# A small early store on the Scalar queue of a DMA-bound softmax

## The chip, the cores and the metric

One core of a Trainium2 chip runs the kernel. The metric is device time in microseconds (us), the median of several executions; most executions of one kernel agree within 0.3%. One traced execution of each kernel gives its profile, whose times count from the start of the span (161.2 us of the 163 us). "Before" is the kernel without the change and "after" the one with it.

## The reference

```python
def setup_inputs():
    batch, seq, dim = 16, 1024, 512
    return {"x": np.random.randn(batch, seq, dim).astype(np.float32)}

def reference(x):
    x_scaled = x / 0.5
    x_max = np.max(x_scaled, axis=-1, keepdims=True)
    exp_x = np.exp(x_scaled - x_max)
    return (exp_x / np.sum(exp_x, axis=-1, keepdims=True)).astype(np.float32)
```

It is a softmax with temperature 0.5 over 16,384 rows of 512 floats: 33.55 MB are read and 33.55 MB written.

## The kernel before

The rows are cut into 8 tiles of 4 MiB. A tile holds 128 partitions with 16 rows each, and those 16 rows lie together in memory, so one partition's share is a run of 32 KiB. Six tiles have buffers. Loads are issued from the Sync engine (SP), stores from the Scalar engine (ACT), one store for each tile.

```python
    FIRST = [(0, 4), (4, 16)]
    data = ctx.enter_context(tc.tile_pool(name="data", bufs=6))
    stats = ctx.enter_context(tc.tile_pool(name="stats", bufs=6))
    ctx.enter_context(tc.manual_schedule())

    warm = stats.tile([P, 1], fp32, name="warm", bufs=1)
    nc.vector.memset(warm, 0.0)
    nc.scalar.activation(out=warm, in_=warm, func=EXP)   # loads ACT's table
    ...
    def load(c):
        xt = tiles[c] = data.tile([P, G, D], fp32, name="xt")
        for lo, hi in FIRST if c == 0 else [(0, G)]:
            nc.sync.dma_start(out=xt[:, lo:hi, :], in_=xr[c][:, lo:hi, :])
    ...
    def store(i):
        c, b = blocks[i]
        if b + B == G:
            nc.scalar.dma_start(out=outr[c], in_=tiles[c])

    for i in range(n + 3):                 # n blocks of 4 rows per partition
        if i < n:
            if blocks[i][1] == 0:
                load(blocks[i][0])
            shift(i)                       # DVE: row maxima
            exponentials(i)                # ACT: exp, in place
        if 1 <= i <= n:
            scale_vector(i - 1)            # DVE: 3 of 4 rows
        if 2 <= i <= n + 1:
            scale_scalar(i - 2)            # ACT: the fourth row
        if 3 <= i:
            store(i - 3)
```

## Time and profile before

| | before |
|---|---|
| time, median of 3 | 162.96 us (162.91 to 163.17) |
| DVE busy / ACT busy | 74% / 71% of the span |
| bytes moved | 67.1 MB |
| first large store issued | 34.23 us |
| its first packets on the 16 DMA engines | 38.6 to 40.4 us |
| last store: first / last of 16 completions | 158.05 / 159.94 us |

These lines of the page of before show the span in 40 slices: first the busy share of the DMA engines in tenths, then what they moved. The two after them give the DMA queues (q1 is SP's, q10 is ACT's; packets, MB, share of the 16 engines' time), and the last two the chain of waits that ended last.

```profile
DMA  5999999998999999999999999999999999999991
GB/s 193 457 463 447 390 463 447 392 455 317 417 472 398 431 472 398 423 480 398 423 472 409 390 488 423 390 488 423 390 488 423 390 488 425 390 480 431 390 480 65
...
q1 hardware_dynamic: 1296, 33.56, 49.2%
q10 hardware_dynamic: 1152, 33.55, 48.2%
...
DMA 54%; DVE 31%; ACT 3%; issue 1%; SPq 0%
DMA xt<-in_x_dram 36%; DVE negmax L65 19%; DMA out_dram<-xt 18%; DVE xt L89 10%; ACT xt L74 2%; DVE bias L67 1%; ACT xt L95 1%; DVE recip L87 1%; SPq L59 0%
```

The DMA engines are busy from the second slice to the last but one: they are the bound. Whatever makes them move less for a moment should therefore be paid at the end.

The GB/s of a slice counts a packet's bytes where the packet starts, and one round of packets on 16 engines is half a megabyte, so neighbouring slices swing between 390 and 488 though nothing happens. For a finer reading I took the trace's DMA packet records and spread each packet's bytes evenly over its duration. Then before moves 433 GB/s in nearly every whole microsecond from 5 to 157 us, with one exception near the tenth slice. Here is that calculation for the microseconds from 34 to 41, in GB/s (the second row is another trace of the same kernel, taken later as an experiment):

```
microsecond      34   35   36   37   38   39   40   41
before          433  428  336  293  321  363  423  429
rep_before      433  433  362  308  310  367  419  426
```

I call this *the hole*. It has a size: the KB missing below 433 GB/s in the ten whole microseconds that follow the issue of the first large store, counted in the packets of the two data queues (q1 and q10) alone. It is 459 and 425 KB in these two traces, about 1.0 us of all 16 engines. In it, 28 to 32 load packets take 1.4 to 2.08 us instead of the usual 1.21 us.

These are the first rows of the timeline of before, and the first store's issue (start, duration, engine, line, what). ACTq and SPq are issues. The Trainium skill (Perfetto Trace Analysis, section on the HWDGE DMA instruction) says that the data movement of a DMA is not inside the reported instruction; this trace agrees: the issue takes 0.37 us and the first packet starts 4.4 us after its start.

```profile
0.72 1.28 ACT L50 ACT_TABLE_LOAD   x1 [0.72 <-PEq L131]
0.73 3.33 SPq L59 DMA_DIRECT2D xt<-in_x_dram  x7
0.80 0.06 DVE L49 MEMSET warm<- 128x1 f32 x1 [0.80 <-PEq L131]
2.02 0.20 ACT L50 ACTIVATE warm<-warm 128x1 f32<-128x1 f32 x1
5.43 2.29 DVE L65 TENSOR_REDUCE negmax<-xt 128x4 f32<-128x2048 f32 x1 [4.58 <-DMA xt<-in_x_dram]
...
34.23 0.37 ACTq L102 DMA_DIRECT2D out_dram<-xt  x1
```

### The profile page before, as it was taken

The page shows a single profiled execution, that of the slowest core. Times are in us where ns is not written, and L with a number is a line of the kernel's source. Part 1 is how long each engine was busy: PE and PEld are TensorE (multiplying, and loading weights), DVE is VectorE, ACT ScalarE, POOL GpSimd, SP SyncE. Part 2 cuts the span into 40 slices and gives each one's busy share as a digit, 9 for nine tenths or more (in the row PEclk, how much of TensorE's full clock was granted, in tenths as well). Part 3 has the DMA queues.
Part 4 walks back from the last instruction along what each step waited for, and adds up shares of the span by engine and source line. Part 5 has one row for each costly group of instructions (what it writes and reads, how often), then busy time and mean ns, then how long its engine had stood idle before and what let it go on. Part 6 is the DMA issues. An engine that isn't in the chain of part 4 may idle for free.

```text
span 161.2 us, 563 instructions
## 1 busy us (share of the span) xinstructions
DVE 119.7 (74%) x193; ACT 114.8 (71%) x290; POOL 0.2 (0%) x4
## 2 busy tenths in 40 slices
DVE  0608999999999999999994999359991799930000
ACT  3072799999999998999995799809997199980000
POOL 0000000000000000000000000000000000000000
DMA  5999999998999999999999999999999999999991
GB/s 193 457 463 447 390 463 447 392 455 317 417 472 398 431 472 398 423 480 398 423 472 409 390 488 423 390 488 423 390 488 423 390 488 425 390 480 431 390 480 65
DMA packets 2452, 67.14 MB, mean 416 GB/s; under 512 B 272, under 2 KB 272, under 8 KB 272
## 3 DMA queue, kind: packets, MB, share of 16 engines
q1 hardware_dynamic: 1296, 33.56, 49.2%
q10 hardware_dynamic: 1152, 33.55, 48.2%
q14 instruction: 4, 0.03, 0.0%
HBM read 33.55 MB, written 33.55 MB: 416 GB/s over the span
## 4 chain that ended last, share of the span: by engine, by line
DMA 54%; DVE 31%; ACT 3%; issue 1%; SPq 0%
DMA xt<-in_x_dram 36%; DVE negmax L65 19%; DMA out_dram<-xt 18%; DVE xt L89 10%; ACT xt L74 2%; DVE bias L67 1%; ACT xt L95 1%; DVE recip L87 1%; SPq L59 0%
## 5 line engine op out<-in xcount | busy, mean ns | idle before, releaser
L74 ACT ACTIVATE xt<-xt,bias 128x512 f32<-128x512 f32 x128 | 90.8, 710 | 28.9 <-DVE bias L67 28.9
L65 DVE TENSOR_REDUCE negmax<-xt 128x4 f32<-128x2048 f32 x32 | 73.0, 2281 | 19.8 <-DMA xt<-in_x_dram 19.8
L89 DVE TENSOR_SCALAR xt<-xt,recip 128x512 f32<-128x512 f32 x96 | 40.9, 483 | 1.1
L74 ACT ACTIVATION_READ_ACCUMULATOR xt<-xt,bias 128x1 f32 x128 | 23.9, 187 | 0.0
L95 ACT ACTIVATE xt<-xt,recip 128x512 f32<-128x512 f32 x32 | 22.4, 706 | 0.0
L87 DVE RECIPROCAL recip<-sums 128x4 f32<-128x4 f32 x32 | 5.5, 171 | 1.6 <-ACT xt L74 1.6
L67 DVE TENSOR_SCALAR bias<-negmax 128x4 f32<-128x4 f32 x32 | 5.5, 170 | 1.1
L50 ACT ACT_TABLE_LOAD x1 | 1.3, 1283 | 0.7 <-PEq L131 0.7
L49 DVE MEMSET warm<- 128x1 f32 x1 | 0.1, 59 | 0.8 <-PEq L131 0.8
L50 ACT ACTIVATE warm<-warm 128x1 f32<-128x1 f32 x1 | 0.2, 203 | 0.0
L131 POOL MEMSET const-bfloat16-1.0<- 128x1 bf16 x1 | 0.1, 101 | 0.0
L131 POOL MEMSET const-uint8-127<- 128x1 uint8 x1 | 0.1, 101 | 0.0
L131 POOL MEMSET const-float32-0.0<- 128x1 f32 x1 | 0.1, 98 | 0.2 <-issue 0.2
L131 POOL MEMSET const-float32-1.0<- 128x1 f32 x1 | 0.1, 98 | 0.0
## 6 DMA issues: line engine op xcount, KB each, us to landing
out_dram<-xt ACTq DMA_DIRECT2D x8, 4096.0 KB, 26.9
xt<-in_x_dram SPq DMA_DIRECT2D x7, 4096.0 KB, 47.3
xt<-in_x_dram SPq DMA_DIRECT2D x1, 3072.0 KB, 11.5
xt<-in_x_dram SPq DMA_DIRECT2D x1, 1024.0 KB, 4.7
```

Source lines behind the costliest of these rows:

```text
L49: nc.vector.memset(warm, 0.0)
L50: nc.scalar.activation(out=warm, in_=warm, func=EXP)
L65: nc.vector.tensor_reduce(negmax, xb, axis=AX, op=MAX, negate=True)
L67: nc.vector.tensor_scalar_mul(bias, negmax, 2.0)
L74: nc.scalar.activation(out=xb[:, g, :], in_=xb[:, g, :], func=EXP, bias=bias[:, g : g + 1], scale=2.0, accum_out=sums[:, g : g + 1],)
L87: nc.vector.reciprocal(recip, sums)
L89: nc.vector.tensor_scalar_mul(xb[:, g, :], xb[:, g, :], recip[:, g : g + 1])
L95: nc.scalar.activation(out=xb[:, g, :], in_=xb[:, g, :], func=COPY, scale=recip[:, g : g + 1])
L131: nc = _bacc.Bacc("TRN2", target_bir_lowering=False, num_devices=1)
```

## The change

The intent is to take the first use of the Scalar queue, with whatever it costs, out of the stretch where the DMA engines are saturated, and put it at the start, where the first load is still on its way.

```diff
+    dram = ctx.enter_context(
+        tc.tile_pool(name="dram", bufs=1, space=bass.MemoryType.DRAM)
+    )
     ctx.enter_context(tc.manual_schedule())
 
+    early = stats.tile([P, 128], fp32, name="early", bufs=1)
+    nc.vector.memset(early, 0.0)
+    scratch = dram.tile([P, 128], fp32, name="scratch")
+    nc.scalar.dma_start(out=scratch, in_=early)
+
     warm = stats.tile([P, 1], fp32, name="warm", bufs=1)
-    nc.vector.memset(warm, 0.0)
-    nc.scalar.activation(out=warm, in_=warm, func=EXP)
+    nc.scalar.activation(out=warm, in_=early[:, 0:1], func=EXP)
```

## The prediction

> **What bounds the kernel now.** The DMA engines. The page's slices show them 90% busy or more from 4 us to the end, for 67.1 MB. Spreading the trace's DMA packet records evenly over their durations gives 433 GB/s in nearly every microsecond from 5 to 157 us. In the table of groups DVE is busy 74% and ACT 71%; in the chain of waits DMA has 54%. The last store is issued at 144.5 us (timeline), while packets of the store before it run to about 150 us: compute has some 4 us of slack.
>
> The one visible hole is at the first store. It is issued on the Scalar queue at 34.23 us, its first packets start at 38.6 to 40.4 us, and meanwhile packets of the loads, 1.21 us for 32 KiB elsewhere, take 1.4 to 2.07 us. The sum falls to 290 to 360 GB/s between 36 and 40 us; about 430 KB is missing, 1.0 us of the 16 engines. It also spreads them: a load's 16 completions lie within 0.43 us before (31.27 to 31.71 us), 2.1 us after (45.5 to 47.6), and the last store's within 1.9 us (158.05 to 159.94). No later issue shows such a hole; both queues then always have work.
>
> **What the change does.** It makes a 64 KiB store the Scalar queue's first DMA, so what the first use costs falls near 1 to 4 us, where the engines are idle until 1.76 us and slow until 3 us (the first load's packets take up to 0.83 us against 0.31 later).
> Added: a memset of 128 columns instead of 1 (0.06 us now, I estimate 0.1 to 0.2); one issue of about 0.34 us on ACT ahead of the 1.28 us table load. ACT is idle until 7.96 us: free. 64 KiB is 0.15 us at 433 GB/s; in 512-byte rows perhaps 0.2 to 0.4 us. The Trainium skill (DMA: Bandwidth & Descriptors, Measured) has 0.95 us of DMA for 64 KB, from another queue; here it overlaps the load.
> Moved: the completion semaphores rotate by one. The sixth full load now waits for the first 1 MiB load (landed by 5.1 us); it was issued near 4 us behind other loads, so nothing is lost.
>
> **How much is critical.** All DMA time. If the hole belongs to the queue's first use, up to 2.1 us on the slowest engine (1.0 mean) leaves 36 to 40 us, and a smaller part, plus 0.2 to 0.4 us for the bytes, appears at the start: net gain 0.5 to 1.8 us. If it belongs to any store that starts on an idle queue while loads stream, it stays, and the change costs 0 to 0.4 us. The Trainium skill (same page, Queues, rings and completion order) gives each queue its own ring on each DMA engine; that does not tell which. I hold the first slightly likelier.
>
> **Predicted:** 162.2 us, 160.7 to 163.6 in 8 of 10 cases; faster by over 2% 0.04, within 2% 0.94, slower by over 2% 0.02.
>
> **What would show it.** Right: the first tile's store starts its packets 1 to 2 us after its issue; load packets around 36 us stay near 1.21 us; the tenth slice rises from 317 GB/s towards 400; the completions near 45 us lie within 1 us. Cost: the first maximum on DVE starts 0.2 to 1 us later than 5.43 us. Wrong: the hole near 36 us stays.
>
> **What would make it wrong.** A hole whenever a store stream begins; a full-size hole at the start, which gives the gain back; an engine left behind by chance.

## The result and the profile after

| | before | after |
|---|---|---|
| time, median | 163.06 us (162.91 to 163.21, 4 runs) | 163.08 us (162.93 to 163.47, 4 runs) |
| ratio | | 1.0005, 95% interval 0.9983 to 1.0027 |
| the 3 MiB load has landed (mean of 16 completions) | 12.07 us | 12.51 us |
| hole at the first large store | 459 KB | 324 KB |
| last store: mean / last of 16 completions | 158.56 / 159.94 us | 158.63 / 159.85 us |

A ratio is the mean time of one kernel's runs over that of the other's of the same rounds, so it is not quite the ratio of the medians quoted. The change does nothing that can be measured: the interval holds 1, and the forecast gain of 0.8 us would have been a ratio of 0.995, outside it.

The same lines of the page of after:

```profile
DMA  5999999999999999999999999999999999999992
GB/s 171 472 415 447 455 398 447 457 398 390 392 472 431 398 472 431 398 463 439 398 455 433 407 464 431 407 463 431 407 455 439 407 439 447 409 439 455 407 423 114
...
q1 hardware_dynamic: 1296, 33.56, 49.1%
q10 hardware_dynamic: 1296, 33.62, 48.4%
...
DMA 54%; DVE 31%; ACT 3%; issue 1%; SPq 0%
DMA xt<-in_x_dram 37%; DVE negmax L74 19%; DMA out_dram<-xt 18%; DVE xt L98 10%; ACT xt L83 2%; DVE bias L76 1%; ACT xt L104 1%; DVE recip L96 1%; SPq L68 0%
```

And its timeline, with the issues of the early store and of the first large store:

```profile
0.73 5.49 SPq L68 DMA_DIRECT2D xt<-in_x_dram  x7
0.82 0.17 DVE L53 MEMSET early<- 128x128 f32 x1 [0.82 <-PEq L140]
1.02 0.36 ACTq L55 DMA_DIRECT2D scratch<-early  x1
1.42 1.28 ACT L59 ACT_TABLE_LOAD   x1 [1.42 <-DVE early L53]
2.71 0.20 ACT L59 ACTIVATE warm<-early 128x1 f32<-128x1 f32 x1
5.90 2.29 DVE L74 TENSOR_REDUCE negmax<-xt 128x4 f32<-128x2048 f32 x1 [4.91 <-DMA xt<-in_x_dram]
...
34.81 0.37 ACTq L111 DMA_DIRECT2D out_dram<-xt  x1
```

The list of DMA issues of after has the early store's size and its time from issue to landing, 5.0 us:

```profile
scratch<-early ACTq DMA_DIRECT2D x1, 64.0 KB, 5.0
```

What was forecast of the added work is there: the memset takes 0.17 us, the issue 0.36 us, the table load ends at 2.70 instead of 2.00 us, and the seventh issue of SP waits for the first load (the seven issues take 5.49 instead of 3.33 us) without harm. The first maximum on DVE starts 0.47 us later.

The tenth slice has gone from 317 to 390 GB/s, which the prediction had named as a sign of success. It is not one. Counted evenly over their durations, the packets of this slice moved 330 GB/s before and 357 after; the rest of the rise comes from where packets start. The second trace of after, rep_after, also has 365 GB/s in this slice by its page, and only 311 when spread evenly. The view of windows for 36 to 40 us (busy times by engine, granted clock, DMA share, GB/s), which also counts packets where they start, says the opposite. Before has 385 GB/s there:

```profile
36.00:40.00 4.00, 3.93 (x7) 3.75 (x10) 0.00 (x0) 1.00 1.13 385
```

The same window of after has 360 GB/s:

```profile
36.00:40.00 4.00, 3.93 (x8) 3.75 (x11) 0.00 (x0) 1.00 1.01 360
```

The packet records, spread evenly, show the hole still there, in this trace and in a second one taken later:

```
microsecond      34   35   36   37   38   39   40   41     hole
after           434  434  419  388  307  324  422  433    324 KB
rep_after       434  434  373  253  264  364  417  434    509 KB
```

The first packets of the large store come 3.9 us after its issue (38.73 us), against 4.4 us before; in the second traces it is the other way round, 4.7 us for rep_after and 4.2 us for rep_before.

### The profile page after: what moved, and what is told of

It is laid out like the page before. It is cut to its first block, busy times and chain, and to the rows that moved or that the text cites. A ratio compares the mean times of both kernels' runs of the same rounds, so it can differ in the third digit from the quotient of the medians.

```text
span 161.2 us, 565 instructions
## 1 busy us (share of the span) xinstructions
DVE 119.8 (74%) x193; ACT 114.8 (71%) x290; POOL 0.2 (0%) x4
## 4 chain that ended last, share of the span: by engine, by line
DMA 54%; DVE 31%; ACT 3%; issue 1%; SPq 0%
DMA xt<-in_x_dram 37%; DVE negmax L74 19%; DMA out_dram<-xt 18%; DVE xt L98 10%; ACT xt L83 2%; DVE bias L76 1%; ACT xt L104 1%; DVE recip L96 1%; SPq L68 0%
```

## The experiments

After the first look there were three theories.

- *A, the first use*: the queue has a price of first use. The early store should have paid it, unless the queue "goes cold" again while it is idle from 5.7 to 34.8 us.
- *B, the joining store*: a hole comes whenever a stream of large stores begins, whatever the queue did before.
- *C, the joining queue*: a hole comes whenever any transfer begins on an empty queue beside a busy one.

In the expectations quoted below "missing" often refers to a fixed stretch such as 32 to 48 us; that is 15 to 30 KB more than the size of the hole as I defined it. Where I give the hole after an early store, it is that of the eight whole microseconds after its issue.

### Both kernels again (rep_before, rep_after)

No edit.

> The kernel before, unchanged, for a second profile: how far the hole at the first store and the spread of completions repeat. In the first profile about 430 KB were missing between 36 and 40 us, load 3's completions ended at 47.6 us and the last store's lay between 158.05 and 159.94 us. If these are a property of the kernel, the hole comes again within 100 KB; if the hole differs by 100 KB or more, the apparent shrinking from 430 to 310 KB in the changed kernel is noise.

> The changed kernel, unchanged, for a second profile and more times. Two profiles of the kernel before miss 482 and 450 KB between 32 and 48 us; the first profile of the changed kernel misses 351 KB there and 318 KB from 2 to 8 us (195 and 211 KB before). If the early store really buys part of the hole and gives it back at the start, this profile again misses about 350 KB at 32 to 48 us. If the smaller hole was chance, it misses about 450 KB. The time is within 0.3% of before either way.

Measured: before again (one run, 163.42 us) has a hole of 425 KB. After again took 163.34 us, ratio 1.0008 (0.9988 to 1.0029), and its hole is 509 KB. So 459 and 425 KB stand against 324 and 509 KB: the smaller hole of the first trace of after was chance. The hole is where it was. The cost at the start does repeat: the mean completion of the 3 MiB load is 12.51 and 12.46 us in the two traces of after, and between 12.07 and 12.26 us in the fourteen traces whose start is that of before: some 0.3 us of delay.

### The small store just before the large one (small_at_25)

```diff
... (early, its memset and scratch as in the change, without the store there)
     for i in range(n + 3):
+        if i == 4:
+            nc.scalar.dma_start(out=scratch, in_=early)   # the same 64 KiB
         if i < n:
```

> The 64 KiB store is moved from the start to about 25 us, so it ends only some 5 us before the first large store. Theory A (the queue was warmed, but goes cold again in the 30 us of idle time that the changed kernel leaves): the hole at 36 to 40 us shrinks to under 150 KB, and a smaller hole of 100 to 300 KB appears around 27 us. Theory B (a hole comes whenever a large store joins on an empty ring while loads stream, whatever went over the ring before): the hole at 36 to 40 us stays at 300 to 430 KB. In both the time is within 0.5% of before.

Measured: 163.18 us, ratio 1.0010 (0.9995 to 1.0025). The small store ends between 35.2 and 36.0 us, more than 12 us after its issue and after the large one has been issued at 34.32 us: its packets take turns with load packets 64 times their size. The hole after its issue is 5 KB, and the hole at the large store is 439 KB. The queue had no time to go cold, and the hole is whole: the cold-queue form of theory A falls.

### A load on the Scalar queue first (load5_on_act)

```diff
-            nc.sync.dma_start(out=xt[:, lo:hi, :], in_=xr[c][:, lo:hi, :])
+            (nc.scalar if c == 5 else nc.sync).dma_start(out=xt[:, lo:hi, :], in_=xr[c][:, lo:hi, :])
...
-            if blocks[i][1] == 0:
+            if i == 3:
+                load(5)
+            if blocks[i][1] == 0 and blocks[i][0] != 5:
```

> The sixth 4 MiB load is issued on the Scalar queue at about 23 us, so this queue has work when the first store is issued behind it at about 34 us. If the hole is the price of a large transfer joining on an empty ring (either direction), it moves to 24 to 29 us and nothing is missing at 34 to 45 us. If it is the price of the first large store (the change of direction), nothing is missing at 24 to 29 us and the hole comes when the store's packets begin, near 43 us. Time within 0.5% of before in either case, since one hole remains.

The issues on the Scalar queue, from the timeline of this run:

```profile
19.18 0.38 ACTq L59 DMA_DIRECT2D xt<-in_x_dram  x1
34.34 0.35 ACTq L102 DMA_DIRECT2D out_dram<-xt  x1
```

Measured: 162.87 us, ratio 0.9987 (0.9970 to 1.0003), which holds 1. The load joins on the empty Scalar queue, its first packet starts at 22.9 us, and the eight microseconds after its issue miss nothing (-1 KB). The store waits behind it in the queue, and the hole comes where the store's packets begin:

```
microsecond      34   35   36   37   38   39   40   41   42   43   44   45
load5_on_act    433  434  434  434  433  430  402  328  295  387  391  409
```

So it is not the queue that joins (theory C falls), nor the queue's first use by packets of 32 KiB: they had just gone through it. It is the first large store.

### The first store in smaller pieces (store0_pieces, rows_16k, rows_8k)

The first store in four stores of 8 KiB per partition:

```diff
-            nc.scalar.dma_start(out=outr[c], in_=tiles[c])
+            for lo in range(0, G, 4 if c == 0 else G):
+                hi = lo + (4 if c == 0 else G)
+                nc.scalar.dma_start(out=outr[c][:, lo:hi, :], in_=tiles[c][:, lo:hi, :])
```

and all transfers with runs of 16 KiB (H = 2) or 8 KiB (H = 4), by another assignment of rows to partitions, with the first tile's loads cut to fit:

```diff
-    xr = xf.rearrange("(c p g) d -> c p g d", p=P, g=G)
+    xr = xf.rearrange("(c h p g) d -> c p h g d", h=H, p=P, g=G // H)
...
-            nc.scalar.dma_start(out=outr[c], in_=tiles[c])
+            nc.scalar.dma_start(out=outr[c], in_=tiles[c].rearrange("p (h g) d -> p h g d", h=H))
```

> The first tile's store is issued as four stores of 4 rows per partition, 8 KiB in a row in place of 32 KiB. If the hole grows with the packet that joins (a fill or hand-over of one packet per engine), it shrinks to under 200 KB and the first store packet comes earlier than 4.4 us after the issue. If it is a fixed latency of the queue, the hole stays at 300 to 430 KB and the first store packet still comes about 4 us after the issue. Time within 0.5% of before.

> Rows are assigned to partitions so that every transfer, load or store, moves pieces of 16 KiB instead of 32 KiB. If the hole is about one store packet per engine, it halves, to 200 to 270 KB at 34 to 48 us. If it is a fixed latency at the change to stores, it stays at 400 to 480 KB. The time is within 0.5% of before: about 0.5 us less for the hole, against a slightly lower rate of smaller packets.

> The same with pieces of 8 KiB for loads and stores. If the hole is about one store packet per engine it falls to a quarter, 90 to 150 KB at 34 to 48 us, and the first store packet comes within about 3 us of its issue. If it is a fixed latency, it stays at 400 to 480 KB. The 8 KiB packets took 309 ns (26.5 GB/s for each engine against 27.0), so the time is expected 1 to 3 us longer.

Measured: store0_pieces 163.29 us, ratio 1.0022 (0.9996 to 1.0048), hole 217 KB; here it is no clean case, because the 8 KiB store packets took turns with 32 KiB load packets, the first store dragged on to 71 us, the loads ran ahead and their queue ran empty at 67 us. rows_16k 163.64 us, ratio 1.0028 (1.0011 to 1.0045), hole 342 KB. rows_8k 164.42 us, ratio 1.0078 (1.0059 to 1.0097), hole 108 KB, below its own level of 424 GB/s (some 80 to 150 KB for levels of 422 to 428, which its rate has before and after). So 8 KiB packets make the hole smaller, by about the three quarters that were expected, and it is not a fixed latency. For 16 KiB half was expected, and 342 KB lies within the 324 to 509 KB of the four traces with 32 KiB packets: one trace does not show that it shrank at all. The first store packet of rows_8k came 3.6 us after its issue, later than the 3 us expected. Neither is faster: the smaller packets run at a lower rate (8 KiB in 309 ns, 16 KiB in 611 ns, 32 KiB in 1213 ns), for the whole run.

### An early store with large packets (big_at_22, big_spread_at_22, same_bytes_4k)

From here on an early store of 512 KiB goes out from the second tile as soon as that has landed, at about 22.5 us:

```diff
+    scratch = dram.tile([16, G, D], fp32, name="scratch")
...
     for i in range(n + 3):
+        if i == 3:
+            load(1)
+            nc.scalar.dma_start(out=scratch, in_=tiles[1][0:16, :, :])      # big_at_22
+            nc.scalar.dma_start(out=scratch, in_=tiles[1][0:P:8, :, :])     # or big_spread_at_22
+            nc.scalar.dma_start(out=scratch, in_=tiles[1][:, 0:2, :])       # or same_bytes_4k, scratch [P, 2, D]
...
-            if blocks[i][1] == 0:
+            if blocks[i][1] == 0 and i != 4:
```

> At about 22 us a store of 16 rows of 32 KiB (512 KiB, one packet of full size for each DMA engine) goes over the Scalar queue to a scratch tensor, and has ended before the first large store. Theory A2 (the first use by packets of full size is what costs): a hole of 300 KB or more at 24 to 30 us and none above 150 KB at 34 to 48 us. Theory B (every time such a store starts on an idle store stream, the engines fall behind by about a packet): 300 to 450 KB missing at 34 to 48 us as before, and a hole of up to that size at 24 to 30 us too. Time: 1.2 us more for the bytes, plus up to 1 us under B.

> As the store of 16 rows of 32 KiB at 22 us, but from partitions 0, 8, 16 and so on in place of 0 to 15. The last run missed 1089 KB at 24 to 32 us, its 16 packets took 2.7 to 4.0 us each, and nothing was missing at the first large store later (38 KB). If the long packets came from 16 neighbouring partitions being read at once, the packets now take under 2.5 us and 350 to 650 KB are missing at 22 to 32 us, while still under 100 KB are missing at the first large store. The time is then about 1 to 1.5 us longer than before (1.2 us of bytes, one hole as before).

> The same 512 KiB at the same place, but as 128 rows of 4 KiB. If the amount that has gone out before counts, the first large store shows no hole (under 100 KB). If the size of a packet counts, most of the hole stays (300 KB or more at the first large store), and 22 to 32 us shows less than 200 KB missing. Time 1.2 to 2.5 us longer than before.

Measured: big_at_22 takes 166.08 us, ratio 1.0184 (1.0160 to 1.0209). Its 16 packets take 2.7 to 4.0 us each and the engines fall to 148 GB/s for two microseconds (1070 KB missing), but at the first large store only 17 KB are missing. big_spread_at_22, which reads from every eighth partition instead of 16 neighbours, takes 164.17 us, ratio 1.0058 (1.0033 to 1.0083): its packets take 1.21 us each, 355 KB are missing after its issue, and 44 KB at the first large store, which is issued at 37.55 us on a queue that has been idle since 30.2 us. Its two first issues on that queue, from the timeline, and its GB/s:

```profile
22.53 0.55 ACTq L112 DMA_DIRECT2D scratch<-xt  x1
37.55 0.38 ACTq L106 DMA_DIRECT2D out_dram<-xt  x1
```

```
microsecond        24   25   26   27   28      38   39   40   41   42   43
big_spread_at_22  369  337  305  370  434     434  433  430  417  427  433
```

This also fells theory B in its plain form: a stream of large stores that begins on an idle queue need not have a hole. same_bytes_4k takes 164.48 us, ratio 1.0083 (1.0053 to 1.0113): 13 KB are missing after its issue and 336 KB at the first large store. The same bytes in small packets do not do it. (An early store also holds ACT up until the second tile has landed, so the first large store comes later, at 36.4 to 44.1 us. That does not remove the hole: same_bytes_4k is the latest of them and has it.)

### Running empty in between (gap_big, gap_only)

Is it then something that is done once, at the first store with large packets? Or a state that holds only while the engines are kept busy? The third load is held back by a small write of DVE to its tile, so that no queue has anything to do for a while, with and without the early store of big_spread_at_22.

```diff
         xt = tiles[c] = data.tile([P, G, D], fp32, name="xt")
+        if c == 2:
+            nc.vector.memset(xt[:, 0, 0:1], 0.0)
...
+        if i == 3:
+            load(1)
+            nc.scalar.dma_start(out=scratch, in_=tiles[1][0:P:8, :, :])    # gap_big only
+        if i == 5:
+            load(2)
+            for c in range(3, 6):
+                load(c)
...
-            if blocks[i][1] == 0:
+            if blocks[i][1] == 0 and blocks[i][0] not in range(1, 6):
```

> As the spread store at 22 us, but the third load is held back by a write of the vector engine to its tile, so that all queues run empty before loads resume; some microseconds later the first large store joins. Theory L (the hole is a lead that the engines' reading takes over their writing, of one large packet, and keeps as long as the queues never run empty): the hole comes back at the first large store, 300 KB or more. Theory F (something is done once, at the first use by a large store packet): under 100 KB are missing at the first large store.

> The same gap without the early store, as a control: both theories expect the hole at the first large store, 300 KB or more missing. If it is missing here too, the gap alone removes it and the run with both says nothing.

The issues in gap_big, from its timeline:

```profile
22.66 0.55 ACTq L114 DMA_DIRECT2D scratch<-xt  x1
28.25 1.95 SPq L65 DMA_DIRECT2D xt<-in_x_dram  x4
34.48 0.38 ACTq L108 DMA_DIRECT2D out_dram<-xt  x1
```

```
microsecond      24   25   26   27   28   29   30   31   32  ...  34   35   36   37   38   39   40
gap_big         211  218   83    0    0  171  272  383  433  ... 433  431  372  329  299  382  434
```

Measured (one run each, 174.97 and 174.53 us, longer by the gap): the early store is over at 26.5 us, nothing moves for the microseconds 27 and 28, loads resume, and at the first large store 372 KB are missing; without the early store 363 KB. In big_spread_at_22, where the loads went on and the Scalar queue alone had been idle for 7 us, it did not come. So it is not something that the first store with large packets does once, whatever goes on around it.

What in gap_big brings the hole back is not shown. Its early store went out alone, because the loads' queue had been empty since 22.3 us; each of its 16 packets took 2.2 to 2.6 us, where those of big_spread_at_22, between load packets, took 1.21 us. So it may never have built what removes the hole, or what it built may have been lost in the gap. Near their end both runs have a second gap, in which no data packet moves from 147.9 to 152.0 us (147.4 to 151.6 in gap_only), and the store after it starts at once with packets of 1.21 to 1.22 us. After an emptiness that long between stores alone, then, no slow packets are seen. A run with the early store between loads and the gap after both would decide it; there is none.

### Grading it (mid_16k_at_22, mid_8k_at_22, one_16k_at_22)

The spread early store again, with other sizes. The one from 32 partitions moves two packets of 16 KiB on each engine, the one from 64 four of 8 KiB, and the third, of only 256 KiB, one of 16 KiB.

```diff
+            nc.scalar.dma_start(out=scratch, in_=tiles[1][0:P:4, 0:8, :])   # mid_16k_at_22
+            nc.scalar.dma_start(out=scratch, in_=tiles[1][0:P:2, 0:4, :])   # or mid_8k_at_22
+            nc.scalar.dma_start(out=scratch, in_=tiles[1][0:P:8, 0:8, :])   # or one_16k_at_22
```

> The spread store of 512 KiB at 22 us in pieces of 16 KiB (32 partitions). The hole at the first large store was about 325 KB after pieces of 4 KiB and under 60 KB after pieces of 32 KiB. Theory L (the lead grows only to the size of the largest store packet so far): two holes that add up to the one of before, about 150 to 250 KB at 22 to 32 us and 150 to 250 KB at the first large store. Theory F2 (only a packet of full size does it, all or nothing): over 350 KB, or under 80 KB, at the first large store. Time about 1 us longer than before either way.

> The same with pieces of 8 KiB (64 partitions). Theory L: 50 to 150 KB missing at 22 to 32 us, 250 to 350 KB at the first large store. All or nothing: as in the run with 16 KiB, no grading.

> 256 KiB in rows of 16 KiB, one packet for each engine, as in prime16_early, but at 22 us and from the tile used by the 512 KiB runs. Theory L graded by what has gone out: about 100 to 150 KB missing at 22 to 32 us and 200 KB or more at the first large store. If instead the effect of the early store wears off (25 us passed in prime16_early, about 11 us in the runs where it held), under 100 KB are missing at the first large store. Time about 0.6 us longer than before.

Measured, in order of what is missing at the early store:

| early store at 22 us | packets on each engine | missing after it | missing at the first large store | sum |
|---|---|---|---|---|
| same_bytes_4k | 8 of 4 KiB | 13 KB | 336 KB | 349 KB |
| one_16k_at_22 | 1 of 16 KiB | 77 KB | 297 KB | 374 KB |
| mid_8k_at_22 | 4 of 8 KiB | 104 KB | 231 KB | 335 KB |
| mid_16k_at_22 | 2 of 16 KiB | 288 KB | 24 KB | 312 KB |
| big_spread_at_22 | 1 of 32 KiB | 355 KB | 44 KB | 399 KB |

The two holes trade against each other, and their sum of 312 to 399 KB is about one hole of a kernel without an early store (324 to 509 KB in the four traces of before and after). Each row is one trace, and 297 and 336 KB are near what an untouched hole can have; the early hole shows the grading more surely, from 13 to 355 KB. The effect is graded, so all-or-nothing falls. But the grading is not the one I expected, "up to the largest packet so far": two packets of 16 KiB already do it all, where half was expected. Times: mid_16k_at_22 164.69 us, ratio 1.0085 (1.0059 to 1.0112; one of its four runs, 170.29 us, was slow and is left out of the ratio); one_16k_at_22 163.41 us, ratio 1.0000 (0.9976 to 1.0024). The single run of mid_8k_at_22, 168.24 us, is of unknown state, and one engine finishes 5 us after the first there; I use its packets up to 50 us and not its time.

### What the packets read (big_first, copy_at_22)

A copy of 16 runs of 32 KiB from the input in HBM to the scratch tensor in HBM, as the very first DMA of the Scalar queue, and again at about 20 us:

```diff
+    scratch = dram.tile([16, G, D], fp32, name="scratch")
+    nc.scalar.dma_start(out=scratch, in_=xr[0][0:16, :, :])                 # big_first, before the warm-up
...
+        if i == 3:
+            load(1)
+            nc.scalar.dma_start(out=scratch, in_=xr[1][0:16, :, :])         # or copy_at_22
```

> The change with packets of full size: the first DMA on the Scalar queue, as early as it can be issued, copies 16 rows of 32 KiB (one packet for each DMA engine) from the input to the scratch tensor in HBM, so that no memset precedes it. Theory L: under 120 KB are missing at 32 to 48 us (450 to 530 KB before), and the start pays instead, 1.2 us for the bytes and up to 1 us more where the engines were not idle anyway; the net time is 0 to 1.5 us longer than before. If the hole at 36 to 40 us stays, a copy that reads HBM does not do what a store from on-chip memory does, and the lead has to do with that reading side.

> The same copy of 512 KiB from the input in HBM to the scratch tensor in HBM as in big_first, but issued near 20 us, where the spread store from on-chip memory removed the later hole. If what counts is that the packets are read from on-chip memory, the hole stays at the first large store (300 KB or more) and 20 to 30 us show under 100 KB missing. If the copy failed in big_first because it came at the start, before the engines were saturated, the hole at the first large store is now under 100 KB.

Measured: big_first takes 164.47 us, ratio 1.0081 (1.0056 to 1.0107), and 353 KB are missing at the first large store. copy_at_22 (one run, 164.92 us) misses 2 KB after its issue and 383 KB at the first large store. Packets of 32 KiB that are written to HBM have no hole and take none away when they are read from HBM. The hole belongs to packets that are read from on-chip memory.

### The change with packets that count (prime16_early)

```diff
+    scratch = dram.tile([16, 8, D], fp32, name="scratch")
+    x0 = data.tile([P, G, D], fp32, name="xt")            # the buffer of the sixth load
+    nc.vector.memset(x0[:, 0:8, :], 0.0)
+    nc.scalar.dma_start(out=scratch, in_=x0[0:P:8, 0:8, :])
...
-        xt = tiles[c] = data.tile([P, G, D], fp32, name="xt")
+        xt = tiles[c] = x0 if c == 5 else data.tile([P, G, D], fp32, name="xt")
```

> The change with a packet of the size that worked: 16 zeroed rows of 16 KiB (256 KiB, one packet for each DMA engine) are stored from on-chip memory at about 5 us, from the buffer that the sixth load fills later. If one packet of 16 KiB on each engine is enough and the engines never run empty after it, 200 to 400 KB are missing at 5 to 14 us and under 100 KB at 34 to 48 us. The net time is then 0.3 to 0.9 us longer than before, since the hole has only moved and the bytes take 0.6 us. If it must be 512 KiB, the hole stays at 36 to 40 us.

Measured: 164.00 us, ratio 1.0038 (1.0013 to 1.0062). The early store is issued at 5.19 us, 135 KB are missing after it (200 to 400 were expected if it worked), and 376 KB at the first large store. One packet of 16 KiB for each engine is too little; one_16k_at_22, with the same amount 14 us before the large store, left 297 KB. Whether the effect also wears off in the 30 us between is not settled: 376 KB is within what an untouched hole has, and also within the scatter around 297.

No run was shown to be faster than both kernels. None of the early stores was a gain: they moved the hole or left it. Most were slower by about their bytes; one_16k_at_22, expected 0.6 us longer, showed no difference.

## Why the prediction was wrong

The time lay in the stated range, 160.7 to 163.6 us, and the large odds on "within 2%" were right. But the middle of the forecast was a gain of 0.8 us (162.2 against 162.96 us), and there was none: 163.08 against 163.06 us.

- *What bounds the kernel*: right. The DMA engines are saturated from about 5 us on, DVE and ACT are not; delays of 0.5 us at the start of the compute did no harm. The Trainium skill (HBM Reference, Specifications (TRN2)) has about 425 GB/s for a core that streams alone, bounded by its 16 DMA engines; the level measured here is 433 GB/s.
- *The hole*: right as a reading. It repeats in a second trace of before (459 and 425 KB) and comes in every other kernel that sent no early store of large packets from on-chip memory.
- *"If the hole belongs to the queue's first use"*: this is the step that failed. The prediction held it slightly likelier than the alternative and built the gain of 0.5 to 1.8 us on it. The runs show that the hole is not the queue's: a load on the same queue has none, and the store behind that load has it all the same (load5_on_act); a small store just before leaves it whole, 439 KB (small_at_25); and the queue can be idle for 7 us without a new hole if a store with large packets has gone before (big_spread_at_22). What the runs put in its place: in a stretch in which loads keep the engines busy, they lose about 300 to 500 KB once, to the first stores whose packets are large and are read from on-chip memory. The 64 KiB of the change go in packets of 512 bytes, and those, like 4 KiB packets, pay next to nothing of it in advance. And had they paid, the sums in the table above suggest that the saving would have been spent in the same coin, at the earlier place.
- *"If it belongs to any store that starts on an idle queue while loads stream, it stays, and the change costs 0 to 0.4 us"*: the outcome of this branch is what came, though its reason is too wide: a store that starts on an idle queue does not always have the hole.
- *The costs*: right. 0.2 to 0.4 us was forecast for the bytes of the early store; the 3 MiB load's mean completion moved from 12.07 to 12.51 us, against 12.07 to 12.26 us in kernels with the old start. Of that, 0.15 us is the bytes at 433 GB/s. At the end of the kernel this is within the scatter of the times. The first maximum starts 0.47 us later, as forecast (0.2 to 1 us). The Trainium skill's 0.95 us for 64 KB (DMA: Bandwidth & Descriptors, Measured), which the prediction took up, is for a load issued from GpSimd, so for another queue and the other direction; this store was spread between load packets from 4.46 to 5.66 us, and what it cost the load is about a third of that.
- *The signs*: the first store's packets were to start 1 to 2 us after its issue; they started after 3.9 us (4.7 us in rep_after). The completions of the fourth full load were to be within 1 us; they lie 1.8 us apart (45.70 to 47.50 us). Both said "wrong". The tenth slice said "right", 390 GB/s for 317, and misled: most of the rise came from where packets start, the rest from a hole that was smaller in this trace and larger in the next.

What stays open is the mechanism inside the DMA engines. A picture that fits is that the reading side of each engine gets ahead of its writing side by some 20 to 30 KB when large store packets come, that this lead is kept as long as the engine has work, and that it has to be built once. Nothing in the records shows the two sides apart, so this is argued and not shown; in this picture it is not clear why a copy from HBM builds no such lead, nor why the stores after the second gap of gap_big start at full speed.

## What to carry to other kernels

Before you pay in advance for a "first use", find out whose first use it is: send the same queue another kind of transfer first, and the same kind of transfer on a warmed queue. In a kernel whose DMA engines are saturated from beginning to end, moving such a loss earlier gained nothing here; it would have to fall where the engines would have been idle, and no run here shows one that did. And look for holes of a microsecond in packet records spread over their durations, in two traces at least: a coarse slice that counts packets where they start rose by 73 GB/s here, and by 40 GB/s between the second traces (325 and 365), though the hole of rep_after was the largest of all four.

## What the Trainium skill lacked or had wrong

- DMA: Bandwidth & Descriptors has no word of a loss when the first stores with large packets join a saturated stream of loads. Here it is 324 to 509 KB (about 1 us of 16 engines) at 32 KiB packets and 108 KB at 8 KiB; it comes in spite of an early store with large packets if that went out alone and all queues were then empty for two to three microseconds (372 KB), and it does not come for a load that joins on an idle queue (-1 KB) or for a copy from HBM to HBM (2 KB).
- The same page (Latency and other measured facts) gives about 600 ns to the first byte on this path. With the engines idle the first load's packets came 1.0 us after the start of the issue (0.73 to 1.76 us); on a queue that joins a busy one, first packets came 3.4 to 4.8 us after it: 3.4 for the first large store of big_spread_at_22, 3.7 for the load at 19.18 us, 4.4 for the first store of before, 4.8 for the early store of big_spread_at_22.
- The same page's rule that engines take turns by packet agrees with the traces, where a packet was a single run, but it does not draw the consequence: 64 KiB in 512-byte packets beside 32 KiB load packets took over 12 us to land (small_at_25, a turn every 1.21 us), and 8 KiB store packets beside 32 KiB load packets let the loads run ahead until their queue was empty at 67 us (store0_pieces).
- The same page's rules say to use 128 partitions for bandwidth. What no page has is a figure for the traffic beside a store that does not: one of 16 runs of 32 KiB from 16 neighbouring partitions held all 16 engines, loads included, at 148 GB/s for two microseconds (packets of 2.7 to 4.0 us), while in the same store from every eighth partition each packet took the usual 1.21 us.
